# Two output projections behind a scan: per token half instead of one after the other

## The chip, the cores and the metric

The kernel runs on one core of one Trainium2 chip. The metric is the device time of one execution in microseconds (us), the median of several runs. The engines are named as in the profile: PE (TensorE matmuls), PEld (its weight loads), DVE (VectorE), ACT (ScalarE), POOL (GpSimd) and SP (SyncE, whose queue issues the DMAs here).

## The reference, cut to what matters

The program is one layer of a bidirectional encoder trunk over 1024 tokens with 1024 channels in float32: a feed-forward half step, a mixer with two branches, a second feed-forward half step, a norm.

```python
merged = jax.nn.sigmoid(g_hy) * y_hy + jax.nn.sigmoid(g_rw) * y_rw
x = x + merged @ w_out
x = x + 0.5 * _swiglu(_rmsnorm(x, ffn2_norm), ffn2_w_gu, ffn2_w_down)
```

`y_rw` is the output of the RWKV-7 branch (two scans, then a projection `@ rw_out` from 512 to 1024 channels). `y_hy` is the output of the Hyena branch. Everything that this document speaks of lies between the end of the scans and the start of the second feed-forward step: the projection with `rw_out`, the gated merge, the projection with `w_out`, the residual add and the RMS norm.

## The kernel before, in words

Activations stand transposed: 128 channels on the partitions, tokens along the free dimension, in two halves of 512 tokens (t = 0 and t = 1). The order of the tokens is permuted by blocks of 128 (`ORDER`), so that the first half holds the middle of the sequence. Each float32 matrix product is made of three float32r matmuls: operands are split into a rounded part (`hi`, written on ACT, L33) and a rest (`lo`, written on DVE or POOL, L37), and `mm3` (L40) multiplies hi by hi (L43), lo by hi (L44) and hi by lo (L45).

`mixer_out` does the work behind the scans. In each half, the first projection (`rw_out`, 512 channels in) has 8 column blocks of 128 channels with 12 matmuls each, from the scan's output `y` (tiles `s_hi`, `s_lo`). A block is then merged on DVE with the gates (`mo_sg`, `mo_mh`; L1623, L1624) and split into `m_hi` and `m_lo`. The second projection (`w_out`, 1024 channels in) has 8 column blocks with 24 matmuls each, from all eight blocks of `m`. L1636 adds its result to the residual `xT`. `done` then squares that block on ACT (`nm_acc`, `nm_sq`) and sums it on DVE (L93). `half_done` closes the norm of a half: the sum's matmuls (`nm_ps`), a short chain of small operations, and for each of eight channel blocks one product on DVE (`nm_h`, L121), its cast on ACT (`hThi`) and its rest (`hTlo`), in turn on DVE and POOL.

In the kernel before, the first projection is done for both halves, then the second for both. `m_hi` and `m_lo` hold 1024 tokens. The scan's output for the second half comes last: the last unit of `post` (`units`, L1605 on) writes it to DRAM (`d_yo`), from where `split_half` (L1456) reads it back (`z_st`) and splits it.

What sets the order: the program text is a list of instructions with priorities in text order, a scheduler (Tile) puts each engine's instructions into one fixed row, and on the chip every engine, and SP's queue, takes its row in order. Buffers come from pools: the staging buffers of all weights (`w_st`, tag shared with `z_st`) are 2, their split forms (`w_hi`, `w_lo`) are 3, the banks for both projections (`mo_ps`) are 4, the gate tiles 2, the buffers `nm_h` 2. `begin()` opens the pools of the second feed-forward step at the place where `early.close()` frees the pools of the scan stage, and reloads the residual `xT` from DRAM with four transfers of 1 MB (L1757).

Of the kernel before, what the change touches and what calls it, by code (L numbers as in the profile page):

```python
# [13 lines left out]
F32 = mybir.dt.float32  # L14
F32R = mybir.dt.float32r
AF = mybir.ActivationFunctionType
ALU = mybir.AluOpType
# [3 lines left out]
P = 128  # L21
L = 1024
# [1532 lines left out]
def mixer_out(tc, I, ident, wp, dr, post, rest, y0, early, begin, done, half_done):  # L1555


    nc = tc.nc
    with ExitStack() as ctx:
        pool = lambda name, bufs, **k: ctx.enter_context(tc.tile_pool(name=name, bufs=bufs, **k))  # L1560
        one = pool("mo1", 1)
        pm = pool("mop", 4, space=PSUM)
        m_hi = one.tile([P, KD, L], F32R, name="m_hi")
        m_lo = one.tile([P, KD, L], F32R, name="m_lo")
        with ExitStack() as c2:
            pool2 = lambda name, bufs, **k: c2.enter_context(tc.tile_pool(name=name, bufs=bufs, **k))
            yb, two = pool2("mo2", 1), pool2("mo3", 2)
            pq = pool2("mopq", 3, space=PSUM)

            def weights(i):  # L1570

                st, hi, lo = [wp.tile([P, KD, P], dt, name=n, tag=n, bufs=b) for n, dt, b in
                              (("w_st", F32, 2), ("w_hi", F32R, 3), ("w_lo", F32R, 3))]
                nc.sync.dma_start(st.rearrange("p (k c) f -> p k (c f)", c=2),
                                  I["rw_out"][:, ts(i, 2 * P)].rearrange("(k p) f -> p k f", p=P))
                split_from(nc, hi, lo, st, "act", "dve")
                return [x.rearrange("p (k c) f -> p k c f", c=2) for x in (hi, lo)]

            merge = {}

            def gates(t, i):

                out = []
                for n in ("sg", "mh"):
                    x = two.tile([P, 2, 512], F32, name="mo_" + n)
                    a = dr[n][ts(i, 2 * P)].rearrange("(j p) (h t) -> p j h t", p=P, t=256)
                    if t == 0:
                        nc.sync.dma_start(x, a[:, :, 1:3].rearrange("p j h t -> p j (h t)"))
                    else:
                        for h in range(2):  # L1590
                            nc.sync.dma_start(x[:, :, ts(h, 256)], a[:, :, 3 * h])
                    out.append(x)
                merge[t, i] = out

            def ahead(n):

                if n < 2 * KD // 2:
                    w.append(weights(n % 4))
                    gates(n // 4, n % 4)

            w = []
            ahead(0)
            post.te, post.work, post.psum = nc.tensor, pool2("mo5", 1), pq
            g = post.load(0, 4)
            units = [rest, post.unit(0, 0, g(0)), post.unit(0, 1, g(1))]  # L1605
            while units:
                units = [u for u in units if next(u, u) is not u]
            y = [y0]
            ahead(1)
            for t in range(2):  # L1610
                if t:
                    y.append(split_half(nc, wp, yb, lambda st, h: nc.sync.dma_start(st, dr["yo"][:, 4:8, 2 * h : 2 * h + 2])))
                for j in range(KD):
                    if j % 2 == 0 and t + j:
                        ahead(4 * t + j // 2 + 1)
                    sg, mh = [x[:, j % 2] for x in merge[t, j // 2]]
                    if j % 2 == 0:
                        w2 = w.pop(0)
                    wj = [x[:, :, j % 2] for x in w2]
                    ps = pm.tile([P, 512], F32, name="mo_ps", tag="mo_ps")  # L1620
                    for k in range(4):
                        mm3(nc, ps, (wj[0][:, k], wj[1][:, k]), (y[t][0][:, k], y[t][1][:, k]), k == 0, k == 3)
                    nc.vector.scalar_tensor_tensor(sg, sg, 1.0, ps, ALU.add, ALU.mult)  # L1623
                    nc.vector.tensor_tensor(sg, sg, mh, ALU.add)  # L1624
                    split_from(nc, m_hi[:, j, ts(t, 512)], m_lo[:, j, ts(t, 512)], sg, "act", "dve")
        early.close()
        xT = begin()
        for t in range(2):
            for j in range(KD):
                w = col_weights(nc, wp, I["w_out"][:, ts(j, P)], KD, lo_eng="dve")  # L1630
                ps = pm.tile([P, 512], F32, name="mo_ps", tag="mo_ps")
                for k in range(KD):
                    mm3(nc, ps, (w[0][:, k], w[1][:, k]), (m_hi[:, k, ts(t, 512)], m_lo[:, k, ts(t, 512)]),
                        k == 0, k == KD - 1)
                xa = xT[:, j, ts(t, 512)]
                nc.vector.scalar_tensor_tensor(xa, ps, 0.5, xa, ALU.mult, ALU.add)  # L1636
                done(j, t)
            half_done(t)


@with_exitstack
# [177 lines left out]
```

## Time and profile before

| | us |
|---|---|
| median of 3 runs | 2841.01 (2840.96 to 2841.77) |
| profiled execution, its own time | 2847.4 |
| span of that execution (first to last instruction) | 2845.6 |
| PE busy in the span | 2715.7 (95%) |
| from the last matmul of the first half's first projection to the end of the second projection | 1956.3 to 2083.6 |

The times of single instructions come from the profiled execution. A row of the timeline gives the start in us from the start of the span, the duration, the engine, the line, the operation with output and inputs, how many were merged into the row, and in brackets the idle time before it with what ended it. Matmuls are pipelined: one with 512 columns is shown as 0.39 to 0.40 us long, but the next one starts 0.227 to 0.233 us later (0.427 us at the lower clock), so starts are what to count by. The same holds on DVE: operations of 128x512 are shown as 0.68 us long and follow each other every 0.60 us.

### The profile page before, as it was taken

The numbers are of one execution on the slowest core, as the hardware profiler recorded it, in microseconds if no ns is written. First come the engines' busy times: TensorE is split into PE (matmuls) and PEld (weight loads), VectorE is DVE, ScalarE is ACT, GpSimd is POOL, SyncE is SP. The second block draws the span as 40 slices with busy tenths as digits, with TensorE's granted clock in tenths as the row PEclk, the third lists the DMA queues.
The fourth block names the chain that finished last, engine by engine and source line by source line (L and its number), as shares of the span: only waits on it lengthen the run. The fifth ranks groups of instructions, "written<-read, shape, count | busy, mean of one in ns | idle before, by whom it ended". The sixth has DMA issues, their size and how long they took to land. (4 is left out here: it accounts for less than half of the span.)

```text
span 2845.6 us, 45944 instructions
## 1 busy us (share of the span) xinstructions
PE 2715.7 (95%) x19440; PEld 2189.7 (77%) x19440; DVE 1215.3 (43%) x2132; ACT 893.4 (31%) x1507; POOL 546.7 (19%) x351
## 2 busy tenths in 40 slices
PE   8999999999988999999999998899999999999998
PEld 6888888888766777776787877776778888888787
DVE  4111010111547769897765767758631110101114
ACT  5111111111444542334554545532331111111113
POOL 2323232232422210000000000000033232332322
PEclk9999999999999999999999999898999999999999
DMA  5111111111341354554544325457521111111102
GB/s 127 56 41 53 44 52 45 49 48 44 112 150 63 105 169 149 173 154 129 173 133 134 104 87 183 144 178 249 151 77 56 48 48 41 56 41 49 49 26 93
DMA packets 402125, 276.43 MB, mean 97 GB/s; under 512 B 50643, under 2 KB 362527, under 8 KB 401280
## 3 DMA queue, kind: packets, MB, share of 16 engines
q1 hardware_dynamic: 401920, 273.50, 31.6%
q8 instruction: 153, 2.51, 0.4%
q14 instruction: 52, 0.43, 0.0%
HBM read 202.53 MB, written 70.91 MB: 96 GB/s over the span
## 5 line engine op out<-in xcount | busy, mean ns | idle before, releaser
L45 PE MATMUL pw<-hThi,w_lo 128*128 128x512 f32 (+1 forms) x1184 | 470.4, 398 | 15.5 <-DVE w_lo L1243 15.5
L43 PE MATMUL pw<-hThi,w_hi 128*128 128x512 f32 (+1 forms) x1184 | 472.2, 399 | 8.1 <-ACT sh_o L1265 4.5
L44 PE MATMUL pw<-hTlo,w_hi 128*128 128x512 f32 (+1 forms) x1184 | 470.8, 398 | 0.0
L33 ACT CAST w_hi<-w_st 128x1024 fp32r<-128x1024 f32 (+1 forms) x168 | 169.5, 1010 | 481.3 <-PE pw L44 185.2
L37 POOL TENSOR_TENSOR w_lo<-w_st,w_hi 128x1024 fp32r<-128x1024 f32 x100 | 239.9, 2399 | 401.0 <-ACT w_hi L33 394.7
L43 PE MATMUL pgu<-hThi,w_hi 128*128 128x512 f32 x704 | 279.1, 397 | 0.8 <-issue 0.8
L44 PE MATMUL pgu<-hTlo,w_hi 128*128 128x512 f32 x704 | 279.1, 396 | 0.3 <-POOL hTlo L37 0.2
L45 PE MATMUL pgu<-hThi,w_lo 128*128 128x512 f32 x704 | 278.9, 396 | 0.0
L43 PE MATMUL pdn<-g_hi,wd_hi 128*128 128x512 f32 x704 | 274.9, 390 | 1.8 <-DVE xT L226 1.7
L44 PE MATMUL pdn<-g_lo,wd_hi 128*128 128x512 f32 x704 | 274.6, 390 | 2.0 <-POOL g_lo L37 2.0
L45 PE MATMUL pdn<-g_hi,wd_lo 128*128 128x512 f32 x704 | 274.8, 390 | 1.7 <-POOL wd_lo L37 1.7
L45 PEld LDWEIGHTS pw<-hThi,w_lo 128*128 128x128 f32 (+1 forms) x1184 | 222.3, 188 | 69.3 <-DVE w_lo L1243 17.7
L43 PEld LDWEIGHTS pw<-hThi,w_hi 128*128 128x128 f32 (+1 forms) x1184 | 222.3, 188 | 63.0 <-ACT sh_o L1265 6.3
L226 DVE SCALAR_TENSOR_TENSOR xT<-pdn,xT 128x512 f32<-128x512 f32 x192 | 132.3, 690 | 314.8 <-PE pdn L45 314.8
L44 PEld LDWEIGHTS pw<-hTlo,w_hi 128*128 128x128 f32 (+1 forms) x1184 | 222.3, 188 | 54.2 <-issue 4.2
L209 DVE TENSOR_TENSOR silu<-silu,pgu 128x512 f32<-128x512 f32 x44 | 30.2, 687 | 449.5 <-PE pgu L45 449.5
L209 DVE TENSOR_TENSOR silu<-silu,pw 128x512 f32<-128x512 f32 x44 | 30.3, 688 | 445.8 <-PE pw L45 445.1
L37 POOL TENSOR_TENSOR wd_lo<-wdst,wd_hi 128x512 fp32r<-128x512 f32 (+1 forms) x112 | 132.1, 1180 | 333.3 <-ACT wd_hi L33 333.3
L37 POOL TENSOR_TENSOR g_lo<-silu,g_hi 128x512 fp32r<-128x512 f32 x88 | 113.5, 1289 | 399.0 <-ACT g_hi L33 399.0
L33 ACT CAST wd_hi<-wdst 128x512 fp32r<-128x512 f32 (+1 forms) x112 | 64.4, 576 | 379.2 <-PE pdn L44 365.7
L37 POOL TENSOR_TENSOR hTlo<-nm_h,hThi 128x512 fp32r<-128x512 f32 x16 | 23.6, 1477 | 737.2 <-ACT hThi L33 737.2
L43 PEld LDWEIGHTS pgu<-hThi,w_hi 128*128 128x128 f32 x704 | 132.4, 188 | 33.1 <-issue 1.2
(316 smaller groups left out, 4423.8 us busy)
## 6 DMA issues: line engine op xcount, KB each, us to landing
w_st<-in_ffn_w_gu SPq DMA_DIRECT2D x88, 512.0 KB, 3.7
w_st<-in_w_in SPq DMA_DIRECT2D x57, 512.0 KB, 3.8
wdst<-in_ffn_w_down SPq DMA_DIRECT2D x64, 256.0 KB, 2.8
wdst<-in_ffn_w_down SPq DMA_DIRECT2D x48, 192.0 KB, 2.5
d_kf<-kout SPq DMA_DIRECT2D x32, 256.0 KB, 2.3
hy_k<-d_kf SPq DMA_DIRECT2D x32, 256.0 KB, 3.1
w_st<-in_w_out SPq DMA_DIRECT2D x16, 512.0 KB, 4.4
d_X<-sh_x SPq DMA_DIRECT2D x12, 512.0 KB, 3.5
```

Of the source, the lines that this page charges most:

```text
L33: nc.scalar.copy(hi, src)
L37: eng.tensor_tensor(lo, src, hi.bitcast(F32), ALU.subtract)
L43: te.matmul(out, lhs[0], rhs[0], start=first, stop=False)
L44: te.matmul(out, lhs[0], rhs[1], start=False, stop=False)
L45: te.matmul(out, lhs[1], rhs[0], start=False, stop=last)
L209: nc.vector.tensor_tensor(sl, sl, pu, ALU.mult)
L226: nc.vector.scalar_tensor_tensor(xa, ps, 0.5, xa, ALU.mult, ALU.add)
```

## The change

The loop over the two halves now holds both projections. For t = 0 the first projection and merge are done, then the pools of the scan stage are closed, the residual is loaded, and the second projection with its norm follows. Then all of this comes for t = 1. `m_hi` and `m_lo` have 512 tokens and one buffer each. The work pool of the last `post` units (`mo5`) is closed as soon as these units are traced.

```diff
-        m_hi = one.tile([P, KD, L], F32R, name="m_hi")
-        m_lo = one.tile([P, KD, L], F32R, name="m_lo")
...
-            post.te, post.work, post.psum = nc.tensor, pool2("mo5", 1), pq
...
+            with tc.tile_pool(name="mo5", bufs=1) as work:
+                post.te, post.work, post.psum = nc.tensor, work, pq
...
             for t in range(2):
                 if t:
                     y.append(split_half(nc, wp, yb, lambda st, h: nc.sync.dma_start(st, dr["yo"][:, 4:8, 2 * h : 2 * h + 2])))
+                m = [one.tile([P, KD, 512], F32R, name=n) for n in ("m_hi", "m_lo")]
                 for j in range(KD):
...
-                    split_from(nc, m_hi[:, j, ts(t, 512)], m_lo[:, j, ts(t, 512)], sg, "act", "dve")
-        early.close()
-        xT = begin()
-        for t in range(2):
-            for j in range(KD):
-                w = col_weights(nc, wp, I["w_out"][:, ts(j, P)], KD, lo_eng="dve")
...
-            half_done(t)
+                    split_from(nc, m[0][:, j], m[1][:, j], sg, "act", "dve")
+                if t == 0:
+                    early.close()
+                    xT = begin()
+                for j in range(KD):
+                    wo = col_weights(nc, wp, I["w_out"][:, ts(j, P)], KD, lo_eng="dve")
+                    ps = pm.tile([P, 512], F32, name="mo_ps", tag="mo_ps")
+                    for k in range(KD):
+                        mm3(nc, ps, (wo[0][:, k], wo[1][:, k]), (m[0][:, k], m[1][:, k]), k == 0, k == KD - 1)
...
+                    done(j, t)
+                half_done(t)
```

Place 1, PE, at the end of the first half's first projection. Names carry a running number; in the row before, `s_hi_17986` is the second half's scan output and `w_hi_17941` the first weight of its first projection.

```order
L45 MATMUL mo_ps_17969<-s_hi_17609,w_lo_17898 128x512
L43 MATMUL mo_ps_18008<-s_hi_17986,w_hi_17941 128x512
L43 MATMUL mo_ps_18025<-s_hi_17986,w_hi_17941 128x512
L44 MATMUL mo_ps_18008<-s_lo_17987,w_hi_17941 128x512
L45 MATMUL mo_ps_18008<-s_hi_17986,w_lo_17942 128x512
```

In the row of the changed kernel, `w_hi_18013` and `w_lo_18014` are the first weight of `w_out`, and `w_hi_18047` is its second.

```order
L45 MATMUL mo_ps_17970<-s_hi_17609,w_lo_17899 128x512
L43 MATMUL mo_ps_18017<-m_hi_17817,w_hi_18013 128x512
L44 MATMUL mo_ps_18017<-m_lo_17818,w_hi_18013 128x512
L43 MATMUL mo_ps_18051<-m_hi_17817,w_hi_18047 128x512
L45 MATMUL mo_ps_18017<-m_hi_17817,w_lo_18014 128x512
L43 MATMUL mo_ps_18017<-m_hi_17817,w_hi_18013 128x512
```

Behind the same last matmul of the first half now stands the second projection of that half. Its third matmul already belongs to the second column block and needs the second weight's `hi`; its fourth needs the first weight's `lo`. The second half's first projection stands 192 matmuls later.

Place 2, SP's queue, around the load of the residual. Before:

```order
L170 DMA w_st<-in_w_out 128x8x128 x2
L1591 DMA mo_mh<-d_mh 128x2x256 x2
L1591 DMA mo_sg<-d_sg 128x2x256 x2
L170 DMA w_st<-in_w_out 128x8x128 x2
L1757 DMA xT<-d_x 128x8x256 x4
L170 DMA w_st<-in_w_out 128x8x128 x12
```

Now:

```order
L1551 DMA d_yo<-rp_y_17659 128x2x256
L1589 DMA mo_mh<-d_mh 128x2x256
L170 DMA w_st<-in_w_out 128x8x128
L1589 DMA mo_sg<-d_sg 128x2x256 x2
L1756 DMA xT<-d_x 128x8x256 x4
L170 DMA w_st<-in_w_out 128x8x128 x2
L1589 DMA mo_sg<-d_sg 128x2x256 x2
L1589 DMA mo_mh<-d_mh 128x2x256 x2
L170 DMA w_st<-in_w_out 128x8x128 x4
L1611 DMA z_st<-d_yo 128x4x256 x2
L1572 DMA w_st<-in_rw_out 128x4x256 x3
```

Four weights of `w_out` were issued ahead of the residual, now two (one more stands further up). The read of the second half's scan output moved from ahead of all of this to behind the first half's eight weights. On ACT the casts of the third and later weights stand behind the squares of the first two blocks (`nm_acc`, `nm_sq`).

Place 3, DVE, where the first half's norm is applied. Before, this stands under the second projection of the second half (`xT_18189` is the residual, `w_lo_18642`, `w_lo_18677` are weights of `w_out`):

```order
L121 SCALAR_TENSOR_TENSOR nm_h_18503<-xT_18189,k_ffn2_norm_75,nm_ps_18490 128x512
L121 SCALAR_TENSOR_TENSOR nm_h_18507<-xT_18189,k_ffn2_norm_75,nm_ps_18490 128x512
L1636 SCALAR_TENSOR_TENSOR xT_18189<-mo_ps_18541,xT_18189 128x512
L37 TENSOR_TENSOR hTlo0_18180<-nm_h_18503,hThi0_18179 128x512
L37 TENSOR_TENSOR w_lo_18642<-w_st_18639,w_hi_18641 128x1024
L121 SCALAR_TENSOR_TENSOR nm_h_18511<-xT_18189,k_ffn2_norm_75,nm_ps_18490 128x512
L121 SCALAR_TENSOR_TENSOR nm_h_18515<-xT_18189,k_ffn2_norm_75,nm_ps_18490 128x512
L37 TENSOR_TENSOR hTlo0_18180<-nm_h_18511,hThi0_18179 128x512
L1636 SCALAR_TENSOR_TENSOR xT_18189<-mo_ps_18575,xT_18189 128x512
```

Now it stands under the first projection and merge of the second half (`w_lo_18456` is the fourth weight of that first projection, needed by its seventh column block):

```order
L37 TENSOR_TENSOR hTlo0_17995<-nm_h_18326,hThi0_17994 128x512
L121 SCALAR_TENSOR_TENSOR nm_h_18334<-xT_18004,k_ffn2_norm_75,nm_ps_18305 128x512
L121 SCALAR_TENSOR_TENSOR nm_h_18338<-xT_18004,k_ffn2_norm_75,nm_ps_18305 128x512
L37 TENSOR_TENSOR m_lo_18361<-mo_sg_18368,m_hi_18360 128x512
L37 TENSOR_TENSOR hTlo0_17995<-nm_h_18334,hThi0_17994 128x512
L1624 TENSOR_TENSOR mo_sg_18368<-mo_sg_18368,mo_mh_18371 128x512
L121 SCALAR_TENSOR_TENSOR nm_h_18342<-xT_18004,k_ffn2_norm_75,nm_ps_18305 128x512
L121 SCALAR_TENSOR_TENSOR nm_h_18346<-xT_18004,k_ffn2_norm_75,nm_ps_18305 128x512
L37 TENSOR_TENSOR m_lo_18361<-mo_sg_18368,m_hi_18360 128x512
L37 TENSOR_TENSOR hTlo0_17995<-nm_h_18342,hThi0_17994 128x512
L37 TENSOR_TENSOR w_lo_18456<-w_st_18454,w_hi_18455 128x1024
L1623 SCALAR_TENSOR_TENSOR mo_sg_18414<-mo_sg_18414,mo_ps_18466 128x512
```

The norm's eight blocks moved from between residual adds to between merges, and all of them stand ahead of the split of that weight.

## Rows read from the trace of the kernel before

**Rows 1.** From the page: busy time of each engine, with its share of the span and its instructions.

```profile
PE 2715.7 (95%) x19440; PEld 2189.7 (77%) x19440; DVE 1215.3 (43%) x2132; ACT 893.4 (31%) x1507; POOL 546.7 (19%) x351
```

**Rows 2.** Busy time in five stretches: start and end, length, busy us of each engine with its instructions, PE's granted clock as a share of full speed, share of the DMA engines, GB/s.

```profile
1956.30:1973.10 16.80, 10.14 (x22) 6.52 (x22) 11.08 (x15) 4.97 (x6) 0.00 (x0) 0.59 0.83 265
1973.10:1990.00 16.90, 16.90 (x76) 13.86 (x76) 15.11 (x22) 7.82 (x10) 0.00 (x0) 1.00 0.74 225
1990.00:2012.00 22.00, 22.00 (x98) 17.99 (x96) 9.86 (x15) 4.96 (x7) 0.00 (x0) 1.00 0.86 267
2012.00:2016.30 4.30, 1.14 (x4) 0.59 (x4) 1.57 (x2) 2.09 (x2) 0.00 (x0) 1.00 0.26 78
2016.30:2083.60 67.30, 67.26 (x302) 54.94 (x301) 43.84 (x57) 24.58 (x34) 11.20 (x6) 1.00 0.37 105
```

**Rows 3.** Timeline of PE from the last matmul of the first half's first projection to the second half's regular pace.

```profile
1955.91 0.50 PE L45 MATMUL mo_ps<-s_hi,w_lo 128*128 128x512 f32 x1
1960.23 1.22 PE L43 MATMUL mo_ps<-s_hi,w_hi 128*128 128x512 f32 x2 [3.82 <-ACT s_hi L33]
1963.37 0.80 PE L44 MATMUL mo_ps<-s_lo,w_hi 128*128 128x512 f32 x1 [1.92 <-DVE s_lo L37]
1963.96 0.63 PE L45 MATMUL mo_ps<-s_hi,w_lo 128*128 128x512 f32 x1
1964.39 0.63 PE L43 MATMUL mo_ps<-s_hi,w_hi 128*128 128x512 f32 x1
...
1968.88 1.22 PE L43 MATMUL mo_ps<-s_hi,w_hi 128*128 128x512 f32 x2 [0.88 <-ACT s_hi L33]
...
1972.87 0.44 PE L45 MATMUL mo_ps<-s_hi,w_lo 128*128 128x512 f32 x1
1973.15 0.39 PE L43 MATMUL mo_ps<-s_hi,w_hi 128*128 128x512 f32 x1
1973.38 0.39 PE L44 MATMUL mo_ps<-s_lo,w_hi 128*128 128x512 f32 x1
```

**Rows 4.** Timeline of DVE over the same gap.

```profile
1957.96 1.22 DVE L37 TENSOR_TENSOR w_lo<-w_st,w_hi 128x1024 fp32r<-128x1024 f32 x1
...
1959.70 1.27 DVE L1623 SCALAR_TENSOR_TENSOR mo_sg<-mo_sg,mo_ps 128x512 f32<-128x512 f32 x2
1960.89 1.28 DVE L1624 TENSOR_TENSOR mo_sg<-mo_sg,mo_mh 128x512 f32<-128x512 f32 x2
1962.10 1.22 DVE L37 TENSOR_TENSOR s_lo<-z_st,s_hi 128x1024 fp32r<-128x1024 f32 x1
1963.23 1.28 DVE L37 TENSOR_TENSOR m_lo<-mo_sg,m_hi 128x512 fp32r<-128x512 f32 x2
```

**Rows 5.** Timeline of SP's queue: when a DMA was issued and how long issuing it (or the merged ones) took.

```profile
1958.07 0.36 SPq L1551 DMA_DIRECT2D d_yo<-rp_y  x1
1958.47 0.47 SPq L1591 DMA_DIRECT2D mo_mh<-d_mh  x1
1959.80 0.87 SPq L1591 DMA_DIRECT2D mo_sg<-d_sg  x2
...
1995.21 7.34 SPq L1757 DMA_DIRECT2D xT<-d_x  x4
```

**Rows 6.** DMA issues between 1930 and 2030 us: count, KB each, median us from issue to landing.

```profile
w_st<-in_w_out SPq DMA_DIRECT2D x11, 512.0 KB, 5.1
xT<-d_x SPq DMA_DIRECT2D x4, 1024.0 KB, 8.5
...
d_yo<-rp_y SPq DMA_DIRECT2D x3, 256.0 KB, 2.2
```

**Rows 7.** Timelines of ACT and PE where the fifth weight of `w_out` was late.

```profile
2009.22 0.63 ACT L92 ACTIVATE nm_sq<-xT 128x512 f32<-128x512 f32 x1 [1.36 <-DVE xT L1636]
2013.65 1.04 ACT L33 CAST w_hi<-w_st 128x1024 fp32r<-128x1024 f32 x1 [3.80 <-DMA w_st<-in_w_out]
...
2014.75 0.50 PE L43 MATMUL mo_ps<-m_hi,w_hi 128*128 128x512 f32 x1 [2.63 <-ACT w_hi L33]
...
2016.01 0.50 PE L45 MATMUL mo_ps<-m_hi,w_lo 128*128 128x512 f32 x1 [0.53 <-DVE w_lo L37]
```

**Rows 8.** Timeline of PE behind a stretch of small matmuls, from the first to the last matmul at the lower clock and the next one.

```profile
1942.24 0.77 PE L43 MATMUL mo_ps<-s_hi,w_hi 128*128 128x512 f32 x1
...
1945.37 0.53 PE L44 MATMUL mo_ps<-s_lo,w_hi 128*128 128x512 f32 x1
1945.74 0.39 PE L45 MATMUL mo_ps<-s_hi,w_lo 128*128 128x512 f32 x1
```

**Rows 9.** The first half's norm. First the instructions on `nm_h` (minimum, median and maximum duration in ns, first and last start), then single rows of the timelines of PE, POOL and DVE.

```profile
L121 DVE SCALAR_TENSOR_TENSOR nm_h<-xT,k_ffn_norm,nm_ps x8: 734/738/748, 2045.0 to 2058.0; 128x512 f32<-128x512 f32 x8
L37 POOL TENSOR_TENSOR hTlo<-nm_h,hThi x4: 1297/1486/2146, 2047.4 to 2059.5; 128x512 fp32r<-128x512 f32 x4
...
2040.51 1.02 PE L104 MATMUL nm_ps<-ones_c,nm_acc 128*128 128x1 f32 x8
...
2047.44 1.35 POOL L37 TENSOR_TENSOR hTlo<-nm_h,hThi 128x512 fp32r<-128x512 f32 x1 [709.08 <-ACT hThi L33]
...
2047.56 2.31 DVE L37 TENSOR_TENSOR w_lo<-w_st,w_hi 128x1024 fp32r<-128x1024 f32 x1
...
2059.27 1.21 DVE L37 TENSOR_TENSOR w_lo<-w_st,w_hi 128x1024 fp32r<-128x1024 f32 x1
```

More of the change, by code (lines that the diff above doesn't have):

```diff
@@ L1602, in mixer_out @@
             ahead(0)
-            post.te, post.work, post.psum = nc.tensor, pool2("mo5", 1), pq
[L1604 to L1607, printed above, removed]
+            with tc.tile_pool(name="mo5", bufs=1) as work:
+                post.te, post.work, post.psum = nc.tensor, work, pq
+                g = post.load(0, 4)
+                units = [rest, post.unit(0, 0, g(0)), post.unit(0, 1, g(1))]
+                while units:
+                    units = [u for u in units if next(u, u) is not u]
             y = [y0]
@@ L1624, in mixer_out @@
                     nc.vector.tensor_tensor(sg, sg, mh, ALU.add)
-                    split_from(nc, m_hi[:, j, ts(t, 512)], m_lo[:, j, ts(t, 512)], sg, "act", "dve")
-        early.close()
-        xT = begin()
-        for t in range(2):
-            for j in range(KD):
-                w = col_weights(nc, wp, I["w_out"][:, ts(j, P)], KD, lo_eng="dve")
[L1631 to L1637, printed above, removed]
-            half_done(t)
+                    split_from(nc, m[0][:, j], m[1][:, j], sg, "act", "dve")
[7 more added lines that the diff above has]
+                        mm3(nc, ps, (wo[0][:, k], wo[1][:, k]), (m[0][:, k], m[1][:, k]), k == 0, k == KD - 1)
+                    xa = xT[:, j, ts(t, 512)]
+                    nc.vector.scalar_tensor_tensor(xa, ps, 0.5, xa, ALU.mult, ALU.add)
+                    done(j, t)
+                half_done(t)
 @with_exitstack
```

## The prediction

> **What bounds the kernel now.** I read the page's busy times first: PE is busy for 95% of the span [rows 1], so PE bounds the kernel, and a change behind the scan can only add or remove PE's waits and its time at the lower clock. Then I cut the part behind the scan into stretches [rows 2]. From 1956.3 to 1973.1 us PE is busy for 10.14 of 16.80 us at a clock of 0.59. From 2012.0 to 2016.3 it is busy for 1.14 of 4.30. Everywhere else up to 2083.6 it has no gap, and in the long last stretch DVE is busy for 43.84 of 67.30 us without PE noticing. Third, PE's timeline in the first of these stretches [rows 3]: it waits 3.82, 1.92 and 0.88 us for the two parts of the second half's scan output, which comes back from DRAM, and runs at the lower of its two levels (1.2 instead of 2.4 GHz, a start every 0.43 us; from 1973.15 on every 0.23) until 1972.87. Taken more finely a matmul starts every 0.427 us at the lower clock, and every 0.233 (first projection) or 0.227 us (second) at the upper. The 22 matmuls of the stretch would have taken 22 x 0.233 = 5.1 us, so this place costs 16.8 - 5.1 = 11.7 us. Fourth, the second gap [rows 7]: 2.63 + 0.53 = 3.2 us, because the fifth weight of w_out lands only then, behind the residual's 4 MB on SP's queue [rows 5]. These 14.9 us are all that can be won here; the count of matmuls stays the same.
>
> **The change part by part.** Three places, each with what it costs before and after.
>
> A, the end of the first half's first projection (1956.3 us). The 3.82, 1.92 and 0.88 us go. What is late next: PE's third matmul there needs the `hi` of w_out's second weight, the fourth the `lo` of the first. On DVE the row is as before up to the merges that end at 1960.89 + 1.28 = 1962.2 [rows 4]; the `s_lo` of 1.22 us is gone, two `m_lo` follow behind their casts (1963.6), and only then the first weight's `lo` (1.14 more), 1964.8. The second weight's DMA needs the staging buffer that the `w_lo` of 1957.96 frees at 1959.2 [rows 4], and stands on SP's queue behind the `mo_mh` of 1958.47 [rows 5]: issued at 1959.3, landed 5.1 us later [rows 6] at 1964.4, cast 1.04 us [rows 7], so PE goes on at 1965.6. Minus two matmuls that run before, PE idles 1965.6 - 1956.3 - 0.5 = 8.8 us. It then starts at the lower clock, as it does after 3.82 us of idleness [rows 3]. Run through without a pause, that lasted from 1942.24 to 1945.7 [rows 8], with pauses from 1963.37 to 1972.87 [rows 3]. I take 4.2 us, nearer to the unbroken case, of which 1 - 0.233/0.427 = 45% is lost: 1.9. A costs 10.7 against 11.7: -1.0. Bounds: 7.9 (released by DVE at 1964.8, no time at the lower clock), -3.8; 15 (weight at 1967.4, 9.5 us of lower clock), +3.3.
>
> B, the third weight of w_out. The residual's load, issued at 1995.21 before, now needs the last matmul on `y` (1956.3), the last `d_yo` landed (1958.07 + 2.2 = 1960.3) and SP free behind `mo_sg` (1959.80 + 0.87 = 1960.7) [rows 5, 6]: 1960.8. Before, the weight behind it was cast 2013.65 - 1995.21 = 18.4 us after that issue [rows 5, 7]. Counted from 1960.8 this gives 1979.2; some 1.5 MB issued just ahead are partly still moving, so I take 1980.6. PE's first two blocks (46 matmuls left, 10.4 us, and the 1.9 of A) end at 1977.9. The cast also stands behind the second block's residual add and square (0.68 and 0.63 us, as the operations in rows 4 and 7), ready at 1979.4, so the DMA decides. Cast, then `lo`, as at 2013.65 to 2016.01 [rows 7]: PE resumes in full at 1982.9, less two matmuls: 4.5 us of waiting against 3.2: +1.3. Bounds: +0.1 (ACT's row decides) to +5.6 (landing at 1983, and the clock falls, 1.9). From then on each weight has a block of 24 x 0.227 = 5.4 us, longer than 5.1 to land, or than cast and `lo` (2.3).
>
> C, the second half's first projection, which now carries the first half's norm. Its scan output is read in time, under the second projection (5.4 us per block). Before, the norm lay under a second projection [rows 9], where DVE has room [rows 2]. Now DVE must, from the start R of this first projection on, and ahead of the `lo` of its fourth weight, do: the `lo` of two weights (2 x 1.14), one norm sum (0.60), twelve merge operations (4 blocks x 3 x 0.60 = 7.2), eight `nm_h` (shown as 0.74, so 0.66 apart: 5.3 [rows 9]), four `hTlo` (2.4), some ten small ones (2.0): 19.8 us, beginning about R + 3 when the third weight is cast, so the end is R + 22.8 if DVE never waits. PE needs that weight at its seventh block: R + 72 x 0.233 + 1.9 for the norm's own small matmuls (1.0 for the sums [rows 9], 0.9 estimated for the spread) + 0.5 = R + 19.2. That is a wait of 3.6 us. DVE will also wait: the third and later norm casts stand on ACT behind the cast of w_out's first weight, which needs the buffer that PE's fourth block frees at about R + 14, and `nm_h` turns through two buffers with a POOL operation of 1.3 to 2.1 us in each turn [rows 9]. Walking that through gives R + 26. I take 4.5 us, nearer to the sum without waits, because in the trace DVE filled such waits with other work. Bounds 0 and 7. PE then falls to the lower clock: 1.9 (0 to 4.3). Two more waits: the norm's sum matmuls stand in PE's row behind the 14th matmul (R + 3.3) while the sum on DVE comes behind the third weight: 1.0 (0 to 2). And when the second projection starts, the last merge's first operation and the `lo` of its weight (0.68 + 1.14, less 0.3) still stand on DVE: 1.5 (0.5 to 2). Before, all this cost nothing (67.26 of 67.30 us busy [rows 2]). C: 4.5 + 1.9 + 1.0 + 1.5 = +8.9, bounds +0.5 and +15.3.
>
> At the end nothing changes: the second half's norm and the first matmuls of the feed-forward step stand in the same order.
>
> Sum: -1.0 + 1.3 + 8.9 = +9.2 us. On the profiled execution's own time, 2847.4 (span 2845.6 and 1.8 around it), that is 2856.6; that execution was 6.4 us above the median of the runs, so on the median 2841.0 + 9.2 = 2850.2, rounded 2850.
>
> **A rule of the Trainium skill.** The row: a `w_lo` that begins 0.12 us behind a POOL `hTlo` took 2.31 us, another with POOL idle 1.21 [rows 9]. The Trainium skill, "SBUF — State Buffer", section "Who interferes with whom", says that a DVE instruction with two SBUF inputs and a GpSimd instruction that reads SBUF take one shared port, the later one being fully blocked until the earlier ends. The trace agrees at this row. By that rule each of the four POOL `hTlo` under C could hold a merge or a `lo` on DVE.
>
> **The rivals.**
> 1. C is hidden: the norm's pieces fall into gaps of DVE and the seventh block's weight is in time. For it: DVE worked through this norm beside three weights in 16.6 us before (2045.0 to 2059.5 + 2.1 [rows 9]). Against it: then there were no merges. A and B alone give -1.0 + 1.3, 2841.3. It decides at C: if DVE ends the weight's `lo` by R + 19.2.
> 2. Not slower, rather faster: the clock. If PE restarts at 1964.8 and at full clock (A at -3.8) and the residual is off the weights' way (B at -3.2, weights early), with C hidden, the sum is -7.0: 2834. One cause could do it: DMA that is faster when the residual moves earlier, at 1960 instead of beside w_out's weights. Against it: 265 GB/s in that stretch already [rows 2].
> 3. The residual blocks the weights for longer: B at +5.6 instead of +1.3, 2854.5. For it: a share of 0.83 of the DMA engines is busy there before the 4 MB are added [rows 2].
> 4. POOL holds DVE four times in C: 4 x (2.31 - 1.21) = 4.4 more, 2854.6 [rows 9].
> That the change does not do what it says is excluded by the engines' rows: the order is as described, and the single buffer of `m_hi` is free before the second half's first merge.
>
> **How the numbers follow.** The forecast (A, B, C as summed) has 0.46, rival 1 0.26, rival 2 0.07, rival 3 0.10, rival 4 0.11. About 0.2% (5.7 us) is what a measurement of this kernel can tell from no change. The forecast, 3 and 4 lie above 2846.7 (0.67); rival 1 within (0.26, and 0.01 of the others), rival 2 below 2835.3 (0.06). The range takes in rival 1 and, above, rivals 3 and 4 with part of C's upper bound: 2838 to 2860. The likeliest case alone spans 2846 to 2855.
>
> **What would show it.** A: PE's first matmul with w_out's first `lo` at 1965 to 1966, an idle time released by `w_hi` or `w_lo` and not by `s_hi`. B: a wait of 3 to 5 us for `w_hi` before the third block. C: a wait of some us for `w_lo` on PE about 20 us into the second half's first projection, with `nm_h` and `hTlo` ahead of it on DVE; a second one of 1 to 2 us when the second projection starts. The forecast is wrong if that wait in C is under 1 us, if PE restarts in A before 1963, or if the second half's first projection lasts less than 25 us.

## The result, and the profile after

| | us |
|---|---|
| median of the changed kernel, 5 runs | 2853.89 (2851.74 to 2860.64) |
| median of the kernel before, 5 runs beside it | 2841.77 (2840.96 to 2846.41) |
| ratio, 95% interval | 1.0042 (1.0027 to 1.0057) |
| profiled execution, its own time | 2853.89 |

The change costs 12.1 us by the medians. Both kernels do the same number of matmuls, and PE is busy as long as before [rows 1]:

```profile
PE 2714.7 (95%) x19440; PEld 2190.3 (77%) x19440; DVE 1214.6 (43%) x2132; ACT 892.9 (31%) x1507; POOL 546.8 (19%) x351
```

To place the loss I cut out one part of the trace, "the part" below: from the first matmul of the first projection to the first matmul (`pgu`) of the feed-forward step. Its busy times, in the columns of [rows 2], for the kernel before:

```profile
1913.38:2084.39 171.01, 159.97 (x676) 124.08 (x677) 114.00 (x181) 53.99 (x74) 11.20 (x6) 0.95 0.61 192
```

For the changed kernel, with the stretches inside it in which PE is idle or at the lower clock:

```profile
1907.20:2090.80 183.60, 160.80 (x676) 125.74 (x677) 113.30 (x181) 53.88 (x74) 11.40 (x6) 0.93 0.57 179
1949.70:1960.20 10.50, 1.01 (x5) 0.54 (x4) 8.85 (x15) 2.88 (x4) 0.00 (x0) 0.71 0.70 203
1960.20:1964.50 4.30, 4.30 (x11) 3.43 (x12) 1.09 (x1) 0.00 (x0) 0.00 (x0) 0.52 1.08 359
1972.70:1977.30 4.60, 0.82 (x3) 0.30 (x2) 2.61 (x3) 2.52 (x3) 0.00 (x0) 1.00 0.99 309
1977.30:1981.60 4.30, 4.27 (x12) 3.35 (x13) 1.23 (x1) 0.20 (x1) 0.00 (x0) 0.60 0.80 241
2010.50:2038.00 27.50, 20.27 (x97) 16.39 (x95) 23.27 (x40) 11.04 (x17) 6.62 (x4) 0.96 0.40 127
2038.00:2042.30 4.30, 4.22 (x10) 3.38 (x11) 2.43 (x5) 1.73 (x3) 0.00 (x0) 0.50 0.53 148
2049.00:2089.90 40.90, 40.90 (x181) 33.60 (x179) 20.22 (x21) 12.45 (x16) 4.78 (x2) 1.00 0.40 116
```

The part is 12.6 us longer, about the whole loss of the medians. (The two profiled executions differ by only 6.5 us, since the part happens to start 6.2 us earlier in that of the changed kernel.) Three places stand still, and the last stretch shows the second projection of the second half without a gap. The timeline of PE in the part, to be held against [rows 3] and [rows 7]:

```profile
1949.64 0.50 PE L45 MATMUL mo_ps<-s_hi,w_lo 128*128 128x512 f32 x1
...
1960.09 0.80 PE L43 MATMUL mo_ps<-m_hi,w_hi 128*128 128x512 f32 x1 [9.49 <-ACT w_hi L33]
...
1964.46 0.39 PE L45 MATMUL mo_ps<-m_hi,w_lo 128*128 128x512 f32 x1
...
1976.07 0.50 PE L43 MATMUL mo_ps<-m_hi,w_hi 128*128 128x512 f32 x1 [3.29 <-ACT w_hi L33]
...
1977.33 0.50 PE L45 MATMUL mo_ps<-m_hi,w_lo 128*128 128x512 f32 x1 [0.53 <-DVE w_lo L37]
...
2015.35 1.02 PE L104 MATMUL nm_ps<-ones_c,nm_acc 128*128 128x1 f32 x8 [0.73 <-issue]
...
2038.08 0.80 PE L45 MATMUL mo_ps<-s_hi,w_lo 128*128 128x512 f32 x1 [6.58 <-DVE w_lo L37]
...
2047.04 0.50 PE L45 MATMUL mo_ps<-m_hi,w_lo 128*128 128x512 f32 x1 [1.01 <-DVE w_lo L37]
```

- A. From 1949.98 to 1964.46 PE makes 12 matmuls in 14.5 us; at 0.227 us they take 2.7. A costs 11.8 us, about as much as the 11.7 in the kernel before.
- B. 3.3 + 0.5 us of waiting, and then 12 matmuls in 4.3 us (granted clock 0.60) instead of 2.7: 5.4 us, against 3.2.
- C. 0.7 + 6.6 + 1.0 us of waiting, and 11 matmuls at the lower clock from 2038.08 to 2042.92, 4.8 us instead of 2.6: 10.6 us, against nothing.

This makes 0.1 + 2.2 + 10.6 = 12.9, against 12.6 measured for the part.

What A and B wait for stands on SP's queue (as in [rows 5]) and in ACT's timeline:

```profile
1952.97 0.37 SPq L170 DMA_DIRECT2D w_st<-in_w_out  x1
...
1954.92 8.46 SPq L1756 DMA_DIRECT2D xT<-d_x  x4
1963.48 5.82 SPq L170 DMA_DIRECT2D w_st<-in_w_out  x2
```

```profile
1958.99 1.04 ACT L33 CAST w_hi<-w_st 128x1024 fp32r<-128x1024 f32 x1 [2.43 <-DMA w_st<-in_w_out]
...
1974.98 1.04 ACT L33 CAST w_hi<-w_st 128x1024 fp32r<-128x1024 f32 x1 [0.80 <-DMA w_st<-in_w_out]
```

The second weight of `w_out` takes 6.0 us from issue to cast; the third, issued behind the residual, takes 11.5. What C waits for is DVE's row; here the rows of DVE and POOL ahead of the fourth weight's `w_lo`, to be held against [rows 9]:

```profile
2024.64 1.41 DVE L121 SCALAR_TENSOR_TENSOR nm_h<-xT,k_ffn_norm,nm_ps 128x512 f32<-128x512 f32 x2 [0.59 <-POOL hTlo L37]
...
2029.03 1.41 DVE L121 SCALAR_TENSOR_TENSOR nm_h<-xT,k_ffn_norm,nm_ps 128x512 f32<-128x512 f32 x2 [1.19 <-POOL hTlo L37]
...
2031.16 1.59 POOL L37 TENSOR_TENSOR hTlo<-nm_h,hThi 128x512 fp32r<-128x512 f32 x1 [2.17 <-ACT hThi L33]
2031.55 1.75 DVE L1624 TENSOR_TENSOR mo_sg<-mo_sg,mo_mh 128x512 f32<-128x512 f32 x1
...
2035.35 1.59 POOL L37 TENSOR_TENSOR hTlo<-nm_h,hThi 128x512 fp32r<-128x512 f32 x1 [2.59 <-ACT hThi L33]
2035.75 2.28 DVE L37 TENSOR_TENSOR w_lo<-w_st,w_hi 128x1024 fp32r<-128x1024 f32 x1
```

DVE waits 0.59 and 1.19 us for an `nm_h` buffer that POOL still reads, and two of its operations beside a POOL `hTlo` take 1.07 us longer than their usual 0.68 and 1.21.

### The profile page after: what moved, and what is told of

It is laid out like the page before. It is cut to its first block, busy times and chain, and to the rows that moved or that the text cites. A ratio compares the mean times of both kernels' runs of the same rounds, so it can differ in the third digit from the quotient of the medians.

```text
span 2852.1 us, 45938 instructions
## 1 busy us (share of the span) xinstructions
PE 2714.7 (95%) x19440; PEld 2190.3 (77%) x19440; DVE 1214.6 (43%) x2132; ACT 892.9 (31%) x1507; POOL 546.8 (19%) x351
## 5 line engine op out<-in xcount | busy, mean ns | idle before, releaser
L45 PE MATMUL pw<-hThi,w_lo 128*128 128x512 f32 (+1 forms) x1184 | 473.3, 400 | 11.7 <-DVE w_lo L1243 11.5
```

The source lines that it names most:

```text
L45: te.matmul(out, lhs[1], rhs[0], start=False, stop=last)
```

## The experiments

Each edit stands on the changed kernel. "The part" is measured as above, in one profiled execution each. "The rest" is what of it lies behind the first half's first projection, counted from the start of that projection's last matmul, where A begins. The ratio is to runs of the kernel before on the same chip.

| run | the part starts at | its length, us | the rest, us | ratio (95%) |
|---|---|---|---|---|
| kernel before | 1913.4 | 171.0 | 128.5 | 1 |
| changed kernel | 1907.2 | 183.6 | 141.2 | 1.0042 (1.0027 to 1.0057) |
| changed kernel again | 1914.5 | 182.8 | 141.0 | 1.0051 (1.0033 to 1.0068) |
| norm late | 1911.3 | 171.8 | 130.0 | 1.0028 (1.0019 to 1.0038) |
| norm late again | 1918.7 | 171.7 | 129.9 | 1.0000 (0.9982 to 1.0018) |
| three `lo` on POOL | 1906.0 | 178.7 | 133.0 | 1.0050 (1.0032 to 1.0069) |
| residual in two portions | 1907.3 | 177.8 | 134.8 | 1.0034 (1.0021 to 1.0048) |
| norm late, three `lo` on POOL, residual in two portions | 1915.3 | 165.6 | 118.6 | 0.9978 (0.9964 to 0.9992) |
| `lo` of three rw_out weights on POOL | 1916.2 | 188.5 | 145.1 | 1.0073 (1.0055 to 1.0090) |
| prefetch late | 1905.8 | 185.6 | 140.6 | 1.0051 (1.0038 to 1.0065) |
| norm late, prefetch late, residual in two portions | 1915.0 | 167.1 | 123.7 | 0.9993 (0.9976 to 1.0010) |
| `hTlo` on DVE | 1907.5 | 180.2 | 138.1 | 1.0034 (1.0016 to 1.0052) |
| norm late, prefetch late, residual in two portions, two weights early | 1910.9 | 158.2 | 113.5 | 0.9941 (0.9917 to 0.9964) |

**How far a single profile can be trusted.** The changed kernel once more, without an edit.

> The changed kernel once more, unchanged, beside the kernels of this call. It gives a second profile and a second ratio. The low-clock stretches of the scan, ahead of the changed part, differ from one execution to the next, so the place at which the first projection starts moves by several us, while the part from there to the first matmul of the feed-forward step (183.6 us in the first profile against 171.0 of the kernel before) should repeat within 2 us: 182 to 186 us, with waits of about 9.5, 3.3 and 6.6 us at the same three places. Ratio 1.003 to 1.0055. If the part differs by more than 3 us between the two profiles, single profiles do not tell the edits apart and only the ratios do.

The part repeats within 0.8 us, with waits of 9.82, 3.67 and 6.58 us at the same places. Its start, behind the same instructions, moves by 7.3 us. So the part tells edits apart to about 1 us, and the ratio only to some 4. The rest repeats within 0.2 us in both pairs of profiles; ahead of it the part also holds the first half's first projection, which took 41.8 to 47.0 us in these runs.

**C: the norm back under the second projection.**

```diff
                 if t == 0:
                     early.close()
                     xT = begin()
+                else:
+                    half_done(0)
...
-                half_done(t)
+                if t:
+                    half_done(t)
```

> The changed kernel, with one thing undone: the first half's norm (its sum matmuls, nm_h, hThi, hTlo) is traced behind the second half's merges, so that it lies under the second half's second projection, as in the kernel before. My theory (C: the norm's DVE work ahead of the split of the fourth rw_out weight makes PE wait): the 6.6 us wait for w_lo in the second half's first projection goes, with it the lower clock behind it (1.9) and the waits of 1.5 + 0.7 + 1.0 us around the norm's small matmuls; the first projection then lasts about 23 us instead of 34.5. What may stay is the 1.0 us at the start of the second projection. Gain 9 to 11 us: 2843 to 2845 us, ratio to the kernel before about 1.001. Rival (the seventh block is late because merges, splits of three weights and casts of the second half are too much for DVE and ACT in this stage by themselves, whatever the norm does): a wait for w_lo or w_hi of 3 us or more stays at the same block, gain 5 us or less: 2849 us or more. Rival 2 (a norm moved later delays the feed-forward step): the wait goes, but 2 us or more come back at the end of the stage.

Between the two ends of the part, all of PE's waits are now those of A and B (the view of waits: what PE waited for, us in total, times, longest; the waits for `rp_y` and of `pgu` are those of its first and last matmul, which the kernel before has too):

```profile
PE mo_ps L43 <- ACT w_hi L33: 13.1, 2, 9.6
PE mo_ps L43 <- DVE rp_y L1549: 2.2, 1, 2.2
PE pgu L43 <- issue: 0.8, 1, 0.8
PE mo_ps L45 <- DVE w_lo L37: 0.5, 1, 0.5
```

The part is 11.8 us shorter, nothing comes back at its end, and it lasts as long as in the kernel before, to within 1 us. The first rival, that merges and splits are too much by themselves, is out. (Of the 1.5 + 0.7 + 1.0 us named in the expectation only the 0.7 is in the part; the other two belong to the second half's norm, behind it.) The ratio, however, fell by less than 11.8 us are worth, so I ran it again.

> The kernel with only the norm moved back under the second projection, once more. In its first profile the part from the start of the first projection to the feed-forward step fell from 183.6 us to 171.8, 11.8 less, but the ratio of the runs fell by only 0.0014 to 0.0023 (4 to 6.6 us). If that difference is chance in the low-clock stretches of the scan ahead of the part, this second profile shows the part at 171 to 173 us again, and the ratio over both calls comes to 1.000 to 1.002. If the edit really gives less (the gain is handed back elsewhere), the part is again 172 us, the ratio stays at 1.002 to 1.004, and the time ahead of the part or behind it is longer by 4 us or more than in the changed kernel.

The part is 171.7 us again, and the ratio 1.0000. The first ratio, 1.0028, does not fit that, though both are of one kernel. The difference does not lie in the part; where it lies is not shown. The starts at 1911.3 and 1918.7 do not explain it: the later one belongs to the lower ratio, in an execution (2853.7 us) that was the slowest of its twelve.

**C: is it DVE's row, or POOL?** First POOL takes three splits off DVE's row.

```diff
-                split_from(nc, hi, lo, st, "act", "dve")
+                split_from(nc, hi, lo, st, "act", lo_eng)
...
-                    w.append(weights(n % 4))
+                    w.append(weights(n % 4, "pool" if n > 4 else "dve"))
```

> The changed kernel; the rest part (lo) of the second, third and fourth rw_out weight of the second half is made on POOL instead of DVE. The norm of the first half stays where the change has put it. Theory 1 (C is DVE's row: the fourth weight's lo stands behind the norm's eight nm_h, their hTlo and the merges): the 6.6 us wait for w_lo in the second half's first projection shrinks to under 2 us. What DVE still has to do then shows up as late merges at the start of the second projection (a wait for m_hi or m_lo of 1 to 4 us), so a gain of 3 to 7 us net: 2847 to 2851. Theory 2 (POOL's own instructions hold DVE, since the two take turns): three more POOL operations of 2.5 us each lengthen DVE operations beside them to about 2.5 us, and the wait stays at 5 us or more or comes back in full one step later: 2853 to 2858.

```profile
2023.46 2.36 POOL L37 TENSOR_TENSOR w_lo<-w_st,w_hi 128x1024 fp32r<-128x1024 f32 x1 [1.12 <-ACT w_hi L33]
2023.94 2.42 DVE L93 TENSOR_TENSOR nm_acc<-nm_acc,nm_sq 128x512 f32<-128x512 f32 x1 [1.55 <-ACT nm_sq L92]
...
2053.39 0.47 PE L43 MATMUL mo_ps<-m_hi,w_hi 128*128 128x512 f32 x1 [2.18 <-ACT m_hi L33]
...
2059.24 0.79 PE L45 MATMUL mo_ps<-m_hi,w_lo 128*128 128x512 f32 x1 [5.15 <-DVE w_lo L37]
```

Both theories hold in part; the gain of 3 to 7 us that I expected did not come. The wait of 6.6 us goes, so the fourth weight's place in DVE's row made it. But it returns one step later, as 2.2 us for `m_hi` and 5.2 us for `w_lo`, because DVE is no sooner done: POOL holds single operations for up to 1.7 us (`nm_acc`, 2.42 instead of 0.68). The waits around the norm's small matmuls grow, too, from 0.7 to 3.3 us. The part grows by 5 to 6 us. Then POOL was left out of the first half's norm.

```diff
-            split_from(nc, hl[t][0][:, k], hl[t][1][:, k], h, "act", "pool" if k % 2 else "dve")
+            split_from(nc, hl[t][0][:, k], hl[t][1][:, k], h, "act", "pool" if k % 2 and not lo_dve else "dve")
...
-            live["nm"].apply(live["xT"], live["nm"].rows(t), t, live["hl"])
+            live["nm"].apply(live["xT"], live["nm"].rows(t), t, live["hl"], t == 0)
```

> The changed kernel; the four hTlo of the first half's norm that are made on POOL are made on DVE. The norm stays under the second half's first projection. In the changed kernel's trace DVE waits 0.6 and 1.2 us there for a POOL hTlo that holds an nm_h buffer, and two DVE operations beside POOL last 1.07 and 1.06 us longer: 3.9 us in all ahead of the fourth weight's lo. Without POOL this goes, and four hTlo of 0.60 us, 2.4 us, come to DVE. Theory 1 (C is DVE's amount of work and its fixed row; POOL adds a little): PE's wait of 6.6 us for w_lo shrinks by 1 to 2 us, to 4.5 to 5.6; total gain 1 to 2 us. Rival (the holds by POOL are what makes C larger than forecast, at 1.1 us each for four): the wait shrinks by 4 us or more, gain 4 us or more. Rival 2 (DVE is full, each operation counts): the wait grows by up to 2.4 us.

```profile
2035.45 0.74 PE L45 MATMUL mo_ps<-s_hi,w_lo 128*128 128x512 f32 x1 [4.45 <-DVE w_lo L37]
...
2047.49 0.50 PE L44 MATMUL mo_ps<-m_lo,w_hi 128*128 128x512 f32 x1 [0.93 <-DVE m_lo L37]
```

The wait shrinks by 2.1 us although DVE has four operations more. The part is 2.6 to 3.4 us shorter, more than my 1 to 2 and less than the rival's 4. POOL's help cost more than it took over, and without it 4.5 us of the wait are left to DVE's own row. Whether the amount of work in that row or only its order makes them is not separated: no run moved the fourth weight's `lo` ahead of the norm on DVE and left all else in place. What speaks for the amount is that in this run DVE worked on behind that `lo` without a pause until 2040.7, and PE still waited 0.93 us for an `m_lo`.

**B: the residual in two portions.** The last two of its four transfers are issued at the start of the second half.

```diff
-            for h in range(4):
-                nc.sync.dma_start(xT[:, :, ts(h, 256)], x_dram[:, :, ts(ORDER[2 * h] // 2, 256)])
+            live["x"] = lambda h: nc.sync.dma_start(xT[:, :, ts(h, 256)], x_dram[:, :, ts(ORDER[2 * h] // 2, 256)])
+            for h in range(2):
+                live["x"](h)
...
                 if t:
+                    more(2)
+                    more(3)
                     y.append(split_half(...
```

> The changed kernel; only the first two of the four 1 MB transfers of the residual are issued where all four were, the other two at the start of the second half, behind the first half's eight w_out weights. My theory of B: the third weight is late because of the residual, but ACT's row (the square of the second block ends at 1974.2, the cast of the third weight at 1975 to 1976) stands right behind it: the cast can come 0.8 us earlier, no more, so PE's wait of 3.3 us shrinks to about 2.5, and the lower clock behind it stays: gain 0.5 to 1.5 us, 2852 to 2853.5. Rival (the residual on the queue is what costs B, all of it): the wait for the third weight goes with its lower clock, gain 4 to 5.5 us, 2848.5 to 2850. Rival 2 (the later 2 MB meet the scan output's read and the rw_out weights of the second half): a wait appears at the start of the second half's first projection, and the kernel is 2 us or more slower than the changed kernel.

I was wrong and the rival right. The wait for the third weight and its lower clock are gone (of PE's waits for a `w_hi` only that of A is left), and the part is 5.0 to 5.8 us shorter. ACT's row did not stay as I had assumed: the scheduler put the third cast ahead of the second block's square, and the weight had landed by then.

```profile
PE mo_ps L43 <- ACT w_hi L33: 9.5, 1, 9.5
...
1969.17 0.63 ACT L89 ACTIVATE nm_acc<-xT 128x512 f32<-128x512 f32 x1 [8.40 <-DMA w_st<-in_w_out]
1969.71 1.04 ACT L33 CAST w_hi<-w_st 128x1024 fp32r<-128x1024 f32 x1
```

**A: an earlier staging buffer, in two ways.** First with three `lo` on POOL (that of the second half's first rw_out weight and of the first two w_out weights).

```diff
-                    w.append(weights(n % 4))
+                    w.append(weights(n % 4, "pool" if n == 4 else "dve"))
...
-                    wo = col_weights(nc, wp, I["w_out"][:, ts(j, P)], KD, lo_eng="dve")
+                    wo = col_weights(nc, wp, I["w_out"][:, ts(j, P)], KD, lo_eng="pool" if t == 0 and j < 2 else "dve")
```

> The changed kernel; the rest part (lo) of three weights is made on POOL instead of DVE: of the second half's first rw_out weight and of the first half's first two w_out weights. Nothing else moves. My theory of A (the second w_out weight is late since its staging buffer came free only when DVE, busy with merges, had split the weight in it): its DMA is issued 4 us or more earlier, before the residual; the 9.5 us of waiting for w_hi at the end of the first half's first projection shrink to 1 to 4 us, and the 1.9 us of lower clock with it or not. But the residual then comes no earlier, and it stands ahead of the fourth w_out weight, so half or more of it may come back as a wait for that weight (B, one block later, 3 to 7 us against 3.3 now): net gain 3 to 6 us, 2848 to 2851 us. Rival (the wait in A is set by the DMA engines being full and not by when the transfer starts): the idle time at 1950 stays above 7 us, gain under 1.5 us. Rival 2 (DVE's merges of the last blocks set it): the wait is released by m_lo or m_hi instead of w_hi and stays above 6 us.

Second by placing the prefetch of that rw_out weight later.

```diff
-                    if j % 2 == 0 and t + j:
+                    if j % 2 == 0 and t + j and (t or j < 6):
                         ahead(4 * t + j // 2 + 1)
...
                 for j in range(KD):
+                    if t == 0 and j == 6:
+                        ahead(4)
```

> The changed kernel; the prefetch of the second half's first rw_out weight (and its gates) is traced at the seventh block of the first half's second projection instead of at the seventh block of its first projection. So the first two w_out weights have both staging buffers early, the second is issued some 15 us earlier than now, and the split of the first stands one step further up on DVE. My theory of A (9.5 us of idle PE because the second w_out weight waits for a staging buffer): PE restarts 4 to 6 us earlier, released by DVE (w_lo or m_lo) and not by w_hi; the third and fourth weights still wait behind the residual on the queue, so B grows by 1 to 4 us. Net gain 2 to 4 us: 2850 to 2852. Rival (in A it is the merges on DVE that end the wait, the weight only arrives at the same time): PE restarts less than 2 us earlier. Rival 2: the later prefetch makes the start of the second half's first projection wait (w_hi of its first weight), loss of 2 us or more there.

PE and ACT with the late prefetch:

```profile
1956.48 0.80 PE L45 MATMUL mo_ps<-m_hi,w_lo 128*128 128x512 f32 x1 [4.29 <-DVE w_lo L37]
...
1974.84 1.04 ACT L33 CAST w_hi<-w_st 128x1024 fp32r<-128x1024 f32 x1 [4.18 <-DMA w_st<-in_w_out]
...
1975.94 0.80 PE L43 MATMUL mo_ps<-m_hi,w_hi 128*128 128x512 f32 x1 [6.67 <-ACT w_hi L33]
```

SP's queue and PE with POOL:

```profile
1950.47 0.41 SPq L170 DMA_DIRECT2D w_st<-in_w_out  x1
...
1957.51 7.78 SPq L1756 DMA_DIRECT2D xT<-d_x  x4
...
1976.72 0.79 PE L43 MATMUL mo_ps<-m_hi,w_hi 128*128 128x512 f32 x1 [7.98 <-ACT w_hi L33]
```

The wait at A shrinks from 9.5 to 4.3 us with the late prefetch, and with POOL it is gone. What comes of it differs, because B is the wait for the first weight of `w_out` that stands behind the residual on SP's queue. With the late prefetch this is still the third: PE stops for it after 48 matmuls of the second projection, as in the changed kernel. It starts again 26.4 us behind the beginning of A in the changed kernel and 25.2 us with the late prefetch, little earlier although the wait at A was 5.2 us shorter, and then runs at the lower clock for some 6 instead of some 3 us. What A gives, B takes, 6.7 us there. The rest is 140.6 us against 141.2 and 141.0: no gain, where I had expected 2 to 4 us. (The part is 2 to 3 us longer for what lies ahead of A, where PE has no wait but a granted clock of 0.89 instead of 0.96; whether the edit did that is not shown.)

With POOL the third weight, issued at 1950.47, gets ahead of the residual, and PE stops for the fourth, after 72 matmuls, as the expectation had said, for 8.0 us, more than the 3 to 7 expected. Here the rest is 8.1 us shorter. Ahead of A some 4 us of this go again, 2.15 of them in a new wait of PE for `rp_k`, where two DVE operations beside POOL's splits took 1.12 and 2.33 us instead of 0.16 and 0.17. The part is 4 to 5 us shorter, but the ratio, 1.0050, shows no gain; that execution was 2848.4 us, near the lower end of its seven (2846.96 to 2867.7). Whether this edit gains by itself is not settled.

**Together.** The first three edits (norm late, `lo` on POOL, residual in two portions).

> The three edits of the other runs of this call together: norm of the first half under the second half's second projection, three lo parts on POOL, residual in two portions. If the causes are independent, the gains add: 9 to 11 for the norm, and for A and B together, now that the residual no longer hands the wait of A on to the next weights, 8 to 14 of the 16.8 us that they cost. So 2829 to 2837 us against 2853.9 of the changed kernel and 2841.8 of the kernel before, ratio 0.996 to 0.998. If A and B are bound by the DMA engines (share above 0.8) and not by the order of the queue, A and B stay at 12 us or more and the time is 2840 to 2845.

As expected, ahead of the kernel before (median 2835.35). But PE still waited 3.2 us for the fourth weight, behind the first half of the residual, and lost 3.3 us in a new place. The rows of POOL, DVE and PE there:

```profile
1951.07 5.17 POOL L37 TENSOR_TENSOR w_lo<-w_st,w_hi 128x1024 fp32r<-128x1024 f32 x2 [611.64 <-DVE rp_y L1545]
1951.62 2.35 DVE L833 TENSOR_SCALAR hr_t<-hr_t 128x8 f32<-128x8 f32 x1
1953.88 2.50 DVE L1547 TENSOR_SCALAR rp_y<-rp_y,k_post 128x256 f32<-128x256 f32 x1
...
1957.27 2.05 PE L844 MATMUL psA<-ident,rp_k 128*128 128x128 f32 x8 [3.29 <-DVE rp_k L837]
```

An operation on 128x8 elements that takes 0.17 us in the changed kernel took 2.35 beside POOL's split. So the next version keeps POOL out: norm late, prefetch late, residual in two portions, each edit as above.

> Three edits to the changed kernel together: the first half's norm under the second half's second projection, the prefetch of the second half's first rw_out weight behind six blocks of the first half's second projection, the residual in two portions. Nothing on POOL, other than in the earlier combination, where two small DVE operations took 2.4 us each beside POOL's splits and PE waited 3.3 us for them. From the start of the first projection to the feed-forward step I expect 160 to 165 us against 183.6 of the changed kernel, 171.0 of the kernel before and 165.6 of the earlier combination. Time 2830 to 2836 us, ratio 0.9955 to 0.998. If A is set by DVE's merges, 6 us of A stay and the part takes 167 to 170 us, ratio about 0.9985.

It has 4.29 us of A left (released by the first weight's `w_lo`) with lower clock behind it, and 1.1 + 0.5 us of B for the third weight, which is again the first behind the residual. The part at 167.1 is shorter than in the kernel before, but over the 165 that I expected, the median of 2841.47 misses the 2830 to 2836, and the ratio does not tell it from the kernel before. A last edit brings that `w_lo` forward:

```diff
+            out_weights = lambda j: col_weights(nc, wp, I["w_out"][:, ts(j, P)], KD, lo_eng="dve")
...
+                    if t == 0 and j in (5, 6):
+                        wos.append(out_weights(len(wos)))
                     sg, mh = [x[:, j % 2] for x in merge[t, j // 2]]
...
-                    wo = col_weights(nc, wp, I["w_out"][:, ts(j, P)], KD, lo_eng="dve")
+                    wo = wos.pop(0) if wos else out_weights(j)
```

> The three edits of the last combination (norm under the second projection, later prefetch of rw_out, residual in two portions) and one more: the first two w_out weights are traced at the sixth and seventh block of the first half's first projection, so that the splits of both stand on DVE ahead of the last merges. PE then works through the first two blocks as the merged channels come, and does not stand still for the 4.3 us wait for w_lo; what is left is DVE's last merge. I expect waits of under 3 us in all at the end of the first projection, of which none is longer than 1.5 us, little or no lower clock behind them, and the part from the first projection to the feed-forward step at 158 to 162 us (167.1 without this edit, 171.0 in the kernel before). Time 2827 to 2834 us, ratio 0.994 to 0.997. If instead the merges get later by the two splits (1.14 us each) and PE waits for m_hi or m_lo for 3 us or more, the part stays at 164 to 168 us.

PE's waits from behind its first matmul of the part to the end of the part:

```profile
PE psA L55 <- DVE rp_y L1520: 1.0, 1, 1.0
PE pgu L43 <- issue: 0.8, 1, 0.8
PE nm_ps L114 <- DVE nm_d L113: 0.8, 1, 0.8
```

None of A, B and C is left, the part takes 158.2 us, 12.8 less than in the kernel before, and the median is 2828.91 us (2825.53 to 2835.35, 6 runs), as expected. The edit did more than bring the `w_lo` forward: SP's queue issues the third and the fourth weight at 1956.50 and 1960.03, ahead of the residual at 1961.17, so the first weight behind it is the fifth, as in the kernel before. This version beats both kernels, with the change's loop over halves in it. No run put the edits to the residual and the weights into the kernel before, so how much of the gain is the loop's is not shown.

## Why the prediction was right

The forecast was 2850.0 us with a range of 2838 to 2860 and slower as the likeliest; the time is 2853.89. The sum of +9.2 stands against 12.9 read from the trace. The range is wide enough to take in rival 1, an unchanged time, so that the time lies in it says little; what bears the forecast out is that the three places and what PE waits for in them were as said. All three terms came out larger than forecast, none made up for another.

- A: forecast 10.7, measured 11.8, so the 1.0 that A was to save did not come. The releaser was the second weight's `w_hi`, as said, and PE ran at the lower clock for 4.4 us (forecast 4.2). The weight took 6.0 us to land, not 5.1. What the forecast did not see is that A and B hang together: shortening A gives nothing while the third weight still stands behind the residual (late prefetch), and gives 8.1 us behind the first projection where the third weight gets ahead of it (POOL).
- B: forecast 4.5, measured 5.4. The DMA decided, as said, by 0.8 us over ACT's row. The waits were smaller (3.8), but the lower clock behind them, which I had put into the upper bound alone, cost 1.6.
- C: forecast 8.9, measured 10.6. The place, the instruction and what stands ahead of it on DVE were as said, and moving the norm back took the loss away. The term that was mis-sized is the wait for the fourth weight's `w_lo`, 4.5 in the forecast and 6.6 measured. The step behind it, that DVE fills its waits with other work, failed: DVE waited 0.6 + 1.2 us for POOL and was held for 2.1. The walk with waits had given R + 26, and PE went on at R + 26.8. (The sum without waits had also counted one weight's `lo` too many: that of the second weight, at 2009.84, was done before R, 2011.28.) The lower clock was 2.3 instead of 1.9, the norm sum 0.7 instead of 1.0, the start of the second projection 1.0 instead of 1.5.
- Rival 1 (C hidden) and rival 2 (faster) fell with the wait of 6.6 us. Rival 3 (the residual blocks weights) had the right mechanism for B, but a price of 2.2, not 5.6. Rival 4 (POOL holds DVE four times) happened twice, at 1.07 us each, not four times, and POOL's buffers cost DVE two waits besides.

The Trainium skill, "SBUF — State Buffer", section "Who interferes with whom", counts `tensor_scalar` in its two-port modes, too, among the DVE operations that a GpSimd instruction can block. The trace of the first combination fits this: a TENSOR_SCALAR of 128x8 that began 0.55 us behind a POOL split took 2.35 us instead of 0.17. In which mode it ran no trace shows.

## What to carry to other kernels

A stage can be moved under other work only if the engine that does it has room there: ask of each of its operations what stands behind it in that engine's row, and which of these PE needs next; here eight `nm_h` and their splits ahead of one weight cost 10.6 of the 12.9 us. Where two waits follow each other and the second is for a load that stands behind a large transfer on the queue, shortening the first gives little or nothing as long as the same load stands there; count how many loads get ahead of that transfer (here two weights in the changed kernel, three with POOL, four in the kernel before and in the last version). An operation given to POOL to relieve DVE can hold DVE for longer than it saves.

## What was not expected

The same instructions ahead of the part bring PE to its start at 1905.8 us in one execution and at 1918.7 in another, while the part itself repeats within 0.8 us. Two measurements of one kernel so gave ratios of 1.0028 (1.0019 to 1.0038) and 1.0000 (0.9982 to 1.0018), intervals that only just fail to meet. The length of the touched stage, read between two instructions that both kernels have, was the sharper measure. What moves its start was not tried.
